# FoX attention: 128 columns in place of 256 for the scores of the first query block and the mixing of the last key block, and no zeros written

## The chip, the cores and the metric

One Trainium2 chip, one core. The metric is the device time of one execution in microseconds (us). The engines are TensorE (PE; its weight loads are listed apart as PEld), VectorE (DVE), ScalarE (ACT), GpSimd (POOL) and SyncE (SP), which issues nearly all DMAs.

## What is computed

A decoder trunk of two layers on 512 tokens of width 1024: layer 0 mixes by forgetting attention, layer 1 by a short gated convolution; each is followed by a squared-ReLU MLP and by gated per-layer embeddings, with RMSNorm around every part. The change touches the attention of layer 0 alone, with 16 heads of width 64 and query blocks of 128:

```python
c = lax.cumsum(log_f, axis=1).transpose(0, 2, 1)
def q_block(i):
    start = i * Q_BLOCK
    ...
    s = jnp.einsum('bhqd,bhkd->bhqk', qb, k, preferred_element_type=jnp.float32)
    s = s + cb[..., :, None] - c[..., None, :]
    s = jnp.where(k_pos[None, :] <= q_pos[:, None], s, NEG_INF)
    pr = jax.nn.softmax(s, axis=-1)
    return jnp.einsum('bhqk,bhkd->bhqd', pr.astype(v.dtype), v)
```

Everything is float32. The mask is causal: query block b sees keys 0 to 128(b+1), and key block j is seen by queries 128j to 512.

## The kernel before, in words

Every float32 operand of a matmul is split in two float32r parts, a rounded one (hi, written by ScalarE at L272) and a residue (lo, written by VectorE, or POOL, at L273); a product is then three matmuls (L264 to L266). In the attention the pieces are stacked so that two matmuls do:

- `scores(h, b)` (L516 on) multiplies query block b of head h with the keys. The stationary operand is the 128 queries, the moving one the keys: `kh` at L524 and `kl` at L525. Only the first n = 128(b+1) columns are wanted, but at least 256 are computed. VectorE adds bias and mask and finds the extremum (L527), ScalarE takes the exponential (L531), VectorE the reciprocal of the sum (L532), POOL multiplies by it (L533).
- `turn(h, j)` transposes the probabilities of key block j for the query blocks j to 3 (L540) and splits them into `ph` and `pl` (L272, L273). For key block 3 only columns 384 to 512 exist. POOL writes zeros to columns 256 to 384 of both (L547), for the mix reads at least 256 columns.
- `mix(h, j)` multiplies the values of key block j (stationary) with `ph` (L562) and `pl` (L563) and accumulates over j in one PSUM bank `ps_o`.

The main loop goes over c, four steps to a head: at each step `turn` for head c//4 and key block c%4, `mix` two steps behind, and `scores` eight steps ahead. Between them it deals out matmuls of the projections of later heads (`qk`) and, in the last heads, of the output projection (`o0_0`, `o1_0` and so on: column half and token block). Weight tiles (`wh`, `wl`) are split ahead of their use, eight tiles ahead as a rule (SOON) and one for the output projection (O_SOON). A scheduler with a timing model of its own then sets the order of the instructions on each engine, save in the last two steps, where TensorE keeps the order of the program. Each engine takes its own queue strictly in order. Bias rows come by DMA (`neg_c`, L510) and POOL masks their diagonal blocks (L511).

At L423, ahead of the attention, the cumulative sum over the tokens is a chain of eight float32r matmuls with a stationary operand of 16 columns and 512, 384, 256 and 128 moving ones.

Of the kernel before, what the change touches and what calls it, by code (L numbers as in the profile page):

```python
# [8 lines left out]
F32 = mybir.dt.float32  # L9
# [6 lines left out]
P = 128  # L16
D = 1024
S = 512
# [4 lines left out]
NB = S // P  # L23
# [45 lines left out]
def trunk(ctx: ExitStack, tc, x, pT, g, wv, wqk, bf, wo, wci, wcq, cw, wco, wup, wdn, wpp, wpg, out):  # L69
    nc = tc.nc  # L70
# [9 lines left out]
    def page(name, dtype=F32):  # L80
        return pages.tile([P, S], dtype, tag="pg", name=name)

    def bank(name):
        return psum.tile([P, S], F32, tag="ps", name=name)

    def stat(name, n=1, dtype=F32):
        return small.tile([P, n], dtype, tag=f"st{n}", name=name, bufs=32 if n == 1 else 8)
# [182 lines left out]
    def split(hi, lo, src, eng=nc.vector):  # L270

        nc.scalar.copy(hi, src)  # L272
        eng.tensor_tensor(out=lo, in0=src, in1=hi.bitcast(F32), op=ALU.subtract)  # L273
# [114 lines left out]
    def attention(hT, first_x, g0, by_hand):  # L388
# [127 lines left out]
        def scores(h, b):  # L516

            q, kh, kl = stacked[h // 2][h % 2]
            n = (b + 1) * P
            nm = max(n, 256)  # L520
            pr = probs[h][b]
            ps = bank(f"sc{h}_{b}")
            qb = q[:, b * P : n]
            nc.tensor.matmul(ps[:, :nm], qb, kh[:, :nm], start=True, stop=False)  # L524
            nc.tensor.matmul(ps[:, :nm], qb, kl[:, :nm], start=False, stop=True)  # L525
            nmx, sm, rs = (stat(f"{s}{h}_{b}") for s in ("nmx", "sm", "rs"))
            nc.vector.tensor_tensor_reduce(  # L527
                out=pr, in0=ps[:, :n], in1=pr, scale=-1.0, scalar=3e38, op0=ALU.add,
                op1=ALU.min, accum_out=nmx,
            )  # L530
            nc.scalar.activation(pr, pr, AF.Exp, bias=nmx, scale=-1.0, accum_out=sm)  # L531
            nc.vector.reciprocal(rs, sm)  # L532
            nc.gpsimd.tensor_scalar(out=pr, in0=pr, scalar1=rs, scalar2=None, op0=ALU.mult)  # L533
# [3 lines left out]
        def turn(h, j):  # L537
            ps = bank(f"pT{h}_{j}")
            for b in range(j, NB):
                nc.tensor.transpose(  # L540
                    ps[:, b * P : (b + 1) * P], probs[h][b][:, j * P : (j + 1) * P], ident
                )
            lo_q = min(j * P, S - 256)
            ph, pl = page(f"ph{h}_{j}", F32R), page(f"pl{h}_{j}", F32R)
            if lo_q < j * P:
                for z in (ph, pl):
                    nc.gpsimd.memset(z[:, lo_q : j * P].bitcast(F32), 0.0)  # L547
            split(ph[:, j * P : S], pl[:, j * P : S], ps[:, j * P :])
            weights[h, j] = (ph, pl)

        def mix(h, j):

            e = h % 2
            if j == 0:
                mixed[h] = bank(f"ps_o{h}")
                if e == 0:
                    outs[h // 2] = page(f"oT{h // 2}")
            ps_o = mixed[h]
            lo_q = min(j * P, S - 256)
            v = vs[j][h // 4][:, h % 4 * P : (h % 4 + 1) * P]  # L560
            ph, pl = weights.pop((h, j))
            nc.tensor.matmul(ps_o[:, lo_q:], v, ph[:, lo_q:S], start=j == 0, stop=False)  # L562
            nc.tensor.matmul(ps_o[:, lo_q:], v, pl[:, lo_q:S], start=False, stop=j == NB - 1)  # L563
            if j == NB - 1:
                a, b = slice(64 * e, 64 * e + 64), slice(64 - 64 * e, 128 - 64 * e)
                o2 = page(f"o2{h}")
                nc.scalar.copy(o2[a, :S], ps_o[b, :])
                nc.vector.tensor_tensor(
                    out=outs[h // 2][a, :S], in0=ps_o[a, :], in1=o2[a, :S], op=ALU.add
                )  # L570
                if e == 1:
                    complete.append(h // 2)
                    split_o()
# [4 lines left out]
        def split_o():  # L578

            if streaming:  # L580
                return
            if not oT:
                oT.append(turned_x)
            while complete:
                k = complete.pop(0)
                split(oT[0].hi[:, k, :], oT[0].lo[:, k, :], outs.pop(k)[:, :S])
# [77 lines left out]
        for c in range(-8, n_sc + LAG):  # L664
            if c == n_sc - BY_HAND:
                by_hand.enter_context(tc.manual_schedule(engines={E.PE}))
            share = 2 * (c + 9) if c < n_sc - 16 else 112 + (c - n_sc + 17) * (28 - LEFT) // (15 + LAG)
            while done < share + AHEAD:
                next(main, None)
                done += 1  # L670
            if 0 <= c < n_sc:
                turn(c // 4, c % 4)
            if c >= LAG:
                mix((c - LAG) // 4, (c - LAG) % 4)
            if c + 8 < n_sc:
                scores((c + 8) // 4, c % 4)
            if c % 4 == 0 and 1 < (c + 8) // 4 + LEAD < H:
                bias((c + 8) // 4 + LEAD)
# [428 lines left out]
```

## Time and profile before

| | |
|---|---|
| median of 3 runs | 1237.49 us (1236.93 to 1237.6) |
| profiled execution, span from first to last instruction | 1235.8 us |
| TensorE busy | 1213.4 us, 98% |
| stage of the change, 78 to 232 us | 154 us, TensorE busy 151.01 |
| zeros on POOL (L547) | 32 instructions, 6.4 us |

The profiled execution shows its span alone; no time of its own around the span is listed, so the median of the runs stands for it. A row of the timeline gives start and duration in us, the engine, the line, the operation, the tiles (out<-in, buffer numbers left out), the stationary shape where there is one, the shape written, and in brackets idle time before it and who ended it. Matmuls overlap, so what one costs TensorE is the step from its start to the next start. In the `out<-in` of a matmul the moving operand stands first, the stationary one second. A row of the table of stages gives the stretch and its length, then the busy time and number of instructions of PE, PEld, DVE, ACT and POOL, the granted clock, the DMA share and GB/s.

### The profile page before, as it was taken

What the parts mean: (1) busy time and instruction counts of PE and PEld (TensorE: products, weight loads), DVE (VectorE), ACT (ScalarE), POOL (GpSimd) and SP (SyncE); (2) the same over time, 40 slices, a digit from 0 to 9 for tenths busy, and PEclk for the clock granted to TensorE, in tenths of its full rate; (3) what the DMA queues carried; (4) which work ended last, traced back from release to release, by engine and by line L of the source; (5) the groups of instructions that cost most, each with busy time, mean ns of one, the idle gap of its engine ahead of it and who ended that gap; (6) DMA issues with size and microseconds to landing.
All of it is one profiled execution on the core that took longest, in us unless ns stands there. A gap on an engine that the chain in (4) does not pass through costs nothing.

```text
span 1235.8 us, 18684 instructions
## 1 busy us (share of the span) xinstructions
PE 1213.4 (98%) x6188; PEld 1030.6 (83%) x6188; DVE 896.5 (73%) x1394; ACT 676.1 (55%) x1429; POOL 686.8 (56%) x667
## 2 busy tenths in 40 slices
PE   7999999999999999999999999999999999999997
PEld 6888888888888888888889999989778888888885
DVE  5657878675667667869877798865767787669873
ACT  5457777556635654465566544445756345635551
POOL 2016667247878777775213255317778868778210
PEclk9999999999999999999999999999999999999999
DMA  7456564442343224428133033552412443235401
GB/s 253 150 160 169 147 159 114 151 164 66 115 137 98 88 88 136 123 69 288 67 102 107 27 107 96 154 176 71 136 59 78 137 136 95 66 114 178 163 18 52
DMA packets 85793, 148.73 MB, mean 120 GB/s; under 512 B 10112, under 2 KB 17328, under 8 KB 85696
## 3 DMA queue, kind: packets, MB, share of 16 engines
q1 hardware_dynamic: 85488, 147.27, 38.7%
q8 instruction: 49, 0.80, 0.3%
q14 instruction: 48, 0.39, 0.1%
q10 hardware_dynamic: 144, 0.26, 0.1%
q0 software_dynamic: 64, 0.00, 0.0%
HBM read 136.93 MB, written 6.37 MB: 116 GB/s over the span
## 4 chain that ended last, share of the span: by engine, by line
PE 89%; DVE 3%; POOL 2%; ACT 2%; issue 2%; DMA 2%; SPq 0%; POOLq 0%; DVEq 0%; ACTq 0%
PE up L266 9%; PE up L265 9%; PE up L264 9%; PE dn L265 8%; PE dn L266 8%; PE dn L264 8%; PE pg L265 2%; PE pg L264 2%; PE pg L266 2%; PE qk L264 2%; PE qk L265 2%; PE qk L266 2%; PE co L264 1%; PE co L266 1%; PE co L265 1%
## 5 line engine op out<-in xcount | busy, mean ns | idle before, releaser
L273 DVE TENSOR_TENSOR wl<-raw,wh 128x512 fp32r<-128x512 f32 (+1 forms) x398 | 370.2, 975 | 27.5 <-ACT wh L272 26.3
L272 ACT CAST wh<-raw 128x512 fp32r<-128x512 f32 (+1 forms) x398 | 217.1, 620 | 4.6 <-DVE xd L348 4.4
L265 PE MATMUL up<-hTh,wl 128*128 128x512 f32 (+1 forms) x576 | 210.2, 365 | 0.0
L266 PE MATMUL up<-hTl,wh 128*128 128x512 f32 (+1 forms) x576 | 209.7, 366 | 0.3 <-DVE hTl L273 0.3
L264 PE MATMUL up<-hTh,wh 128*128 128x512 f32 (+1 forms) x576 | 209.4, 366 | 0.0
L273 POOL TENSOR_TENSOR wl<-dn_T,wh 128x512 fp32r<-128x512 f32 x112 | 155.0, 1417 | 32.6 <-ACT wh L272 32.6
L825 ACT ACTIVATE r<-up 128x512 f32<-128x512 f32 (+1 forms) x72 | 39.4, 547 | 200.4 <-PE up L266 200.4
L871 DVE TENSOR_TENSOR acc<-dn,acc 128x512 f32<-128x512 f32 x168 | 107.2, 678 | 23.9 <-PE dn L266 23.9
L265 PEld LDWEIGHTS up<-hTh,wl 128*128 128x128 f32 x576 | 108.6, 189 | 17.7
L264 PEld LDWEIGHTS up<-hTh,wh 128*128 128x128 f32 x576 | 108.6, 189 | 17.5
L266 PEld LDWEIGHTS up<-hTl,wh 128*128 128x128 f32 x576 | 108.3, 189 | 17.9 <-DVE hTl L273 0.5
L167 POOL TENSOR_TENSOR dn_T<-raw,raw 128x512 f32<-128x512 f32 x56 | 87.5, 1575 | 58.9 <-DMA raw<-in_wdn 39.6
L167 POOL TENSOR_TENSOR dn_T<-raw,dn_T 128x512 f32<-128x512 f32 x56 | 93.3, 1666 | 2.2
L272 ACT CAST wh<-dn_T 128x512 fp32r<-128x512 f32 x112 | 61.4, 616 | 11.0 <-POOL dn_T L167 11.0
L273 DVE TENSOR_TENSOR A12l<-q,A12h 128x512 fp32r<-128x512 f32 x28 | 23.3, 833 | 51.7 <-ACT A12h L272 51.7
L273 DVE TENSOR_TENSOR A11l<-q,A11h 128x256 fp32r<-128x256 f32 x28 | 25.9, 926 | 45.5 <-ACT A11h L272 45.5
L878 POOL TENSOR_TENSOR acc<-acc,acc 128x512 f32<-128x512 f32 x28 | 46.9, 1706 | 9.9 <-DVE acc L871 9.9
L264 PE MATMUL qk<-hTh,wh 128*128 128x512 f32 x128 | 51.1, 399 | 0.0
L266 PE MATMUL qk<-hTl,wh 128*128 128x512 f32 x128 | 50.8, 397 | 0.0
L265 PE MATMUL pg<-wh,hTl 128*128 128x512 f32 x128 | 50.5, 394 | 0.0
L264 PE MATMUL pg<-wh,hTh 128*128 128x512 f32 x128 | 50.4, 394 | 0.0
L265 PE MATMUL qk<-hTh,wl 128*128 128x512 f32 x128 | 50.2, 393 | 0.0
(372 smaller groups left out, 3240.3 us busy)
## 6 DMA issues: line engine op xcount, KB each, us to landing
raw<-in_wup SPq DMA_DIRECT2D x128, 256.0 KB, 3.0
raw<-in_wdn SPq DMA_DIRECT2D x128, 256.0 KB, 2.9
raw<-in_wcq SPq DMA_DIRECT2D x36, 256.0 KB, 2.9
raw<-in_wqk SPq DMA_DIRECT2D x32, 256.0 KB, 3.6
raw<-in_wpg SPq DMA_DIRECT2D x32, 256.0 KB, 4.0
g<-in_g SPq DMA_DIRECT2D x22, 256.0 KB, 5.8
prl<-neg_c SPq DMA_DIRECT2D x16, 256.0 KB, 7.0
raw<-in_wo SPq DMA_DIRECT2D x16, 256.0 KB, 4.0
```

Of the source, the lines that this page charges most:

```text
L167: ins = nc.gpsimd.tensor_tensor(out=B[name], in0=B[a], in1=B[b], op=op)
L264: nc.tensor.matmul(ps, a.hi, b.hi, start=start, stop=False)
L265: nc.tensor.matmul(ps, a.lo, b.hi, start=False, stop=False)
L266: nc.tensor.matmul(ps, a.hi, b.lo, start=False, stop=stop)
L272: nc.scalar.copy(hi, src)
L273: eng.tensor_tensor(out=lo, in0=src, in1=hi.bitcast(F32), op=ALU.subtract)
L825: nc.scalar.activation(r[:, :n], ps[:, :n], AF.Relu)
L871: nc.vector.tensor_tensor(out=a, in0=banks[s], in1=a, op=ALU.add)
L878: nc.gpsimd.tensor_tensor(out=a, in0=a, in1=acc[i, s][:, :S], op=ALU.add)
```

## The change

The score matmuls of query block 0 and the mixing matmuls of key block 3 take 128 columns, and the zeros are not written.

```diff
             n = (b + 1) * P
-            nm = max(n, 256)
...
-            nc.tensor.matmul(ps[:, :nm], qb, kh[:, :nm], start=True, stop=False)
-            nc.tensor.matmul(ps[:, :nm], qb, kl[:, :nm], start=False, stop=True)
+            nc.tensor.matmul(ps[:, :n], qb, kh[:, :n], start=True, stop=False)
+            nc.tensor.matmul(ps[:, :n], qb, kl[:, :n], start=False, stop=True)
...
-            lo_q = min(j * P, S - 256)
             ph, pl = page(f"ph{h}_{j}", F32R), page(f"pl{h}_{j}", F32R)
-            if lo_q < j * P:
-                for z in (ph, pl):
-                    nc.gpsimd.memset(z[:, lo_q : j * P].bitcast(F32), 0.0)
...
-            lo_q = min(j * P, S - 256)
+            q0 = j * P
...
-            nc.tensor.matmul(ps_o[:, lo_q:], v, ph[:, lo_q:S], start=j == 0, stop=False)
-            nc.tensor.matmul(ps_o[:, lo_q:], v, pl[:, lo_q:S], start=False, stop=j == NB - 1)
+            nc.tensor.matmul(ps_o[:, q0:], v, ph[:, q0:S], start=j == 0, stop=False)
+            nc.tensor.matmul(ps_o[:, q0:], v, pl[:, q0:S], start=False, stop=j == NB - 1)
```

Lines behind the edits move up: L524 and L525 become L523 and L524, L540 becomes L539, L562 and L563 become L557 and L558. The scheduler then sets some instructions in another order. Three places follow, first before and then after the change; the last number of each name is only a count.

TensorE, mix of head 6, key blocks 2 and 3 (`ph6_2` to `pl6_3`), with scores of head 9 and transpositions of head 7; before:

```order
L563 MATMUL ps_o6_2166<-pl6_2_2163,v2_1_141 128x256
L524 MATMUL sc9_1_2272<-kh4_1_1720,qs4_1_1719 128x256
L525 MATMUL sc9_1_2272<-kl4_1_1721,qs4_1_1719 128x256
L562 MATMUL ps_o6_2166<-ph6_3_2189,v3_1_145 128x256
L563 MATMUL ps_o6_2166<-pl6_3_2190,v3_1_145 128x256
L540 MATMUL pT7_2_2292<-ident_75,prr7_1789 128x128
```

And after:

```order
L558 MATMUL ps_o6_2154<-pl6_2_2151,v2_1_141 128x256
L557 MATMUL ps_o6_2154<-ph6_3_2177,v3_1_145 128x128
L523 MATMUL sc9_1_2258<-kh4_1_1714,qs4_1_1713 128x256
L558 MATMUL ps_o6_2154<-pl6_3_2178,v3_1_145 128x128
L524 MATMUL sc9_1_2258<-kl4_1_1715,qs4_1_1713 128x256
L539 MATMUL pT7_2_2278<-ident_75,prr7_1781 128x128
```

The mix of key block 3 stands two and one matmuls earlier, between the scores of head 9; the set of matmuls is the same.

POOL at the zeros of head 6, which stand behind the normalizing of head 8's third query block (`prr8`) and ahead of the fourth's (`prl8`); before:

```order
L533 TENSOR_SCALAR pr4_1936<-pr4_1936,rs8_1_2134 128x256
L533 TENSOR_SCALAR prr8_1938<-prr8_1938,rs8_2_2175 128x384
L547 MEMSET ph6_3_2189 128x128
L547 MEMSET pl6_3_2190 128x128
L533 TENSOR_SCALAR prl8_1937<-prl8_1937,rs8_3_2202 128x512
```

And after:

```order
L511 AFFINE_SELECT prl9_2074<-prl9_2074 128x128
L532 TENSOR_SCALAR pr4_1926<-pr4_1926,rs8_1_2122 128x256
L532 TENSOR_SCALAR prr8_1928<-prr8_1928,rs8_2_2163 128x384
L532 TENSOR_SCALAR prl8_1927<-prl8_1927,rs8_3_2188 128x512
L511 AFFINE_SELECT prr10_2222<-prr10_2222 128x128
```

The two zeros are gone, and nothing else on POOL is moved there.

VectorE in the last heads, where residues of the output weights (`wl63`, `wl64`) stand among the softmax steps of head 15 (`ISA` is the row of L527); before:

```order
L273 TENSOR_TENSOR pl13_3_3160<-pT13_3_3157,ph13_3_3159 128x128
L273 TENSOR_TENSOR wl63_3178<-raw63_3179,wh63_3177 128x512
L532 RECIPROCAL rs15_1_3114<-sm15_1_3113 128x1
L527 ISA prr15_2971,nmx15_2_3141<-sc15_2_3138,prr15_2971 128x384
L527 ISA nmx15_2_3141 128x1
L273 TENSOR_TENSOR pl14_0_3192<-pT14_0_3186,ph14_0_3191 128x512
L273 TENSOR_TENSOR wl64_3198<-raw64_3199,wh64_3197 128x512
L532 RECIPROCAL rs15_2_3143<-sm15_2_3142 128x1
L527 ISA prl15_2970,nmx15_3_3170<-sc15_3_3167,prl15_2970 128x512
```

And after:

```order
L273 TENSOR_TENSOR pl13_3_3134<-pT13_3_3131,ph13_3_3133 128x128
L531 RECIPROCAL rs15_1_3088<-sm15_1_3087 128x1
L526 ISA prr15_2947,nmx15_2_3115<-sc15_2_3112,prr15_2947 128x384
L526 ISA nmx15_2_3115 128x1
L273 TENSOR_TENSOR wl63_3150<-raw63_3151,wh63_3149 128x512
L273 TENSOR_TENSOR pl14_0_3164<-pT14_0_3158,ph14_0_3163 128x512
L531 RECIPROCAL rs15_2_3117<-sm15_2_3116 128x1
L526 ISA prl15_2946,nmx15_3_3142<-sc15_3_3139,prl15_2946 128x512
L526 ISA nmx15_3_3142 128x1
L273 TENSOR_TENSOR wl64_3170<-raw64_3171,wh64_3169 128x512
```

Each residue stands one softmax step later.

## Prediction

> **What bounds the kernel now.** I began with the head of the page: its span, the busy times, the granted clock and the shares of the chain that ended last.
>
> ```profile
> span 1235.8 us, 18684 instructions
> PE 1213.4 (98%) x6188; PEld 1030.6 (83%) x6188; DVE 896.5 (73%) x1394; ACT 676.1 (55%) x1429; POOL 686.8 (56%) x667
> PEclk9999999999999999999999999999999999999999
> PE 89%; DVE 3%; POOL 2%; ACT 2%; issue 2%; DMA 2%; SPq 0%; POOLq 0%; DVEq 0%; ACTq 0%
> ```
>
> TensorE is busy for 98% of the span, at its full granted clock in every slice, and carries 89% of the chain. A change is therefore worth what it takes from TensorE's own time, plus what it takes from TensorE's few waits. POOL is busy for 56%, so zeros that it no longer writes count only where somebody waited for them.
>
> Next I cut out the stage of the change, from just before the first scores to the last mix, with the table of stages.
>
> ```profile
> 78.00:232.00 154.00, 151.01 (x808) 127.77 (x808) 120.64 (x340) 111.39 (x277) 97.96 (x152) 1.00 0.54 141
> ```
>
> The columns are PE, PEld, DVE, ACT and POOL. TensorE is busy for 151.0 of 154 us here, so most of its matmuls simply follow one another, and about 3 us of idle time is all that shorter waits could give.
>
> **The matmuls that get shorter.** There are 64: for each of 16 heads the two score matmuls of query block 0 (L524, L525) and the two mixing matmuls of key block 3 (L562, L563), each 256 columns before and 128 now. The group rows say 281 to 320 ns for such a 256-column matmul, but those durations overlap; the cost to TensorE is the step from one start to the next. I read it from the timeline of PE, first where three 256-column score matmuls stand together.
>
> ```profile
> 81.58 0.28 PE L525 MATMUL sc<-kl,qs 128*128 128x256 f32 x1
> 81.69 0.28 PE L524 MATMUL sc<-kh,qs 128*128 128x256 f32 x1
> 81.81 0.28 PE L525 MATMUL sc<-kl,qs 128*128 128x256 f32 x1
> 81.94 0.34 PE L524 MATMUL sc<-kh,qs 128*128 128x384 f32 x1
> ```
>
> From 81.58 to 81.94 three of them take 0.36 us: 0.12 us each. No 128-column matmul of this type with a 128x128 stationary operand stands in the trace. The nearest is the cumulative sum at L423, with a stationary operand of only 16 columns; its rows on PE, then the weight loads beside it.
>
> ```profile
> 47.96 0.22 PE L423 MATMUL ps_c<-tri,lf_h 128*16 128x128 f32 x1
> 48.02 0.22 PE L423 MATMUL ps_c<-tri,lf_l 128*16 128x128 f32 x1
> 48.08 0.44 PE L264 MATMUL v<-wh,hTh 128*128 128x512 f32 x1
> 48.36 0.39 PE L265 MATMUL v<-wh,hTl 128*128 128x512 f32 x1
> 48.59 0.39 PE L266 MATMUL v<-wl,hTh 128*128 128x512 f32 x1
> ```
>
> ```profile
> 48.02 0.19 PEld L264 LDWEIGHTS v<-wh,hTh 128*128 128x128 f32 x1
> 48.13 0.19 PEld L265 LDWEIGHTS v<-wh,hTl 128*128 128x128 f32 x1
> ```
>
> This gives both ends. The stream itself is short: 0.06 us from 47.96 to 48.02, again to 48.08, so 128 columns run at full speed. But the next matmul has 128x128 weights. Their load began with the second short matmul, at 48.02, and the following load could begin only at 48.13; the 512-column matmul recorded at 48.08 took 0.28 us to the next start, where its neighbour took 0.23. The missing 0.05 us is a load that the short stream does not cover. So a 128-column matmul followed by a 128x128 load costs the load: 0.11 us. A second place says the same, where a 128-column transposition runs ahead of a score matmul.
>
> ```profile
> 104.80 0.19 PEld L524 LDWEIGHTS sc<-kh,qs 128*128 128x128 f32 x1
> 104.91 0.19 PEld L525 LDWEIGHTS sc<-kl,qs 128*128 128x128 f32 x1
> ```
>
> Again 0.11 us from load to load. In the attention every matmul has a stationary operand of 128 columns (queries, values, normalized tokens, probabilities), so each of the 64 stands ahead of such a load. The bounds are 0.06 us (no load in the way) and 0.11 us; I take 0.11, the row with the same neighbour. **Gain: 64 x (0.12 - 0.11) = 0.64 us**; by the other end 64 x 0.06 = 3.84 us. Halving the columns is worth almost nothing by itself.
>
> The Trainium skill, "TensorE: Matmul & The Clock Gate", section "Back-to-back issue gap", gives about 81 ns per matmul for a stream of load and matmul pairs at 128 columns; by it the sum of this part would be 64 x 0.039 = 2.5 us, an estimate from that page. The rows above, 0.11 us from load to load, do not agree with it.
>
> **The zeros.** POOL writes them with 32 instructions (L547), here in groups.
>
> ```profile
> L547 POOL MEMSET pl<- 128x128 f32 x16 | 3.2, 203 | 0.0
> L547 POOL MEMSET ph<- 128x128 f32 x16 | 3.2, 203 | 0.0
> ```
>
> They go. Off POOL's 97.96 busy us that alone is nothing, but the mix of key block 3 needs both zeroed strips, and the strips are queued behind POOL's normalizing of a later head (L533). Three times TensorE came to that mix first. PE around head 1:
>
> ```profile
> 113.43 0.27 PE L540 MATMUL pT<-ident,prr 128*128 128x128 f32 x1
> 113.46 0.37 PE L563 MATMUL ps_o<-pl,v 128*128 128x256 f32 x1
> 113.67 0.27 PE L540 MATMUL pT<-ident,prl 128*128 128x128 f32 x1
> 114.49 0.39 PE L562 MATMUL ps_o<-ph,v 128*128 128x256 f32 x1 [0.56 <-POOL ph L547]
> 114.72 0.28 PE L524 MATMUL sc<-kh,qs 128*128 128x256 f32 x1
> ```
>
> A transposition and a 256-column matmul normally take 0.24 us together (113.43 to 113.67). Here they took 1.05 (113.67 to 114.72): 0.81 us lost. Heads 6 and 10:
>
> ```profile
> 161.15 0.28 PE L525 MATMUL sc<-kl,qs 128*128 128x256 f32 x1
> 162.01 0.39 PE L562 MATMUL ps_o<-ph,v 128*128 128x256 f32 x1 [0.59 <-POOL ph L547]
> 162.24 0.31 PE L563 MATMUL ps_o<-pl,v 128*128 128x256 f32 x1
> ```
>
> ```profile
> 198.85 0.28 PE L563 MATMUL ps_o<-pl,v 128*128 128x256 f32 x1
> 199.70 0.39 PE L562 MATMUL ps_o<-ph,v 128*128 128x256 f32 x1 [0.58 <-POOL ph L547]
> 199.93 0.27 PE L540 MATMUL pT<-ident,prr 128*128 128x128 f32 x1
> ```
>
> Two 256-column steps normally take 0.23 us (81.58 to 81.81). Here 1.09 and 1.08: 0.86 and 0.85 us lost. What POOL did ahead of the first:
>
> ```profile
> 113.05 1.24 POOL L533 TENSOR_SCALAR prr<-prr,rs 128x384 f32<-128x384 f32 x1
> 114.24 0.20 POOL L547 MEMSET ph<- 128x128 f32 x1
> ```
>
> The zeros waited for a 1.24 us normalization with which they have nothing to do. What would be late next? The probabilities themselves: VectorE's 128x128 residue is the last other input of that mix.
>
> ```profile
> 110.88 0.28 DVE L273 TENSOR_TENSOR pl<-pT,ph 128x128 fp32r<-128x128 f32 x1
> 158.08 0.29 DVE L273 TENSOR_TENSOR pl<-pT,ph 128x128 fp32r<-128x128 f32 x1 [0.29 <-ACT ph L272]
> 198.10 1.22 DVE L273 TENSOR_TENSOR pl<-pT,ph 128x256 fp32r<-128x256 f32 x3
> ```
>
> For heads 1 and 6 it ends at 111.16 and 158.37, 2.5 us and more before TensorE arrives. For head 10 it is the middle one of three merged instructions, which end at 199.32 at the latest; the new order takes only the rounded part right after 198.85 and the residue after two transpositions, so at most some 0.1 us could remain. The whole wait should go. **Gain: 0.81 + 0.86 + 0.85 = 2.52 us**, between 0 (another wait takes their place) and 2.52.
>
> **Moved instructions.** With the zeros gone, the scheduler sets the mix of key block 3 one or two matmuls earlier in most heads, as the order at head 6 shows; the same matmuls, so the sum of their steps stays, and the inputs lie 2.5 us back. On ScalarE, VectorE and SyncE a few weight splits and loads move behind steps of the softmax; weights are prepared up to eight tiles ahead of their use, and in the last heads, where it is one tile, the matmuls that use them move back too. So I cost this at nothing. If that cover were gone, a late weight would stop TensorE for one 128x512 split, well under 1 us each.
>
> **Sum.** 0.64 + 2.52 = 3.16 us. The span of 1235.8 goes to about 1232.6. What lies around the span is 1237.49 - 1235.8 = 1.7 us by the median of the runs; it stays. Forecast: 1237.49 - 3.16 = **1234.3 us**.
>
> **Rivals.** *The waits come back later.* TensorE, 2.5 us ahead, could run into the softmax of the last heads, where the other engines set the pace.
>
> ```profile
> 205.00:210.00 5.00, 5.00 (x32) 4.22 (x31) 2.23 (x8) 2.02 (x6) 3.25 (x7) 1.00 0.39 110
> 210.00:215.00 5.00, 4.57 (x28) 3.50 (x28) 4.88 (x16) 4.92 (x14) 5.00 (x9) 1.00 0.02 3
> 215.00:220.00 5.00, 5.00 (x28) 3.97 (x28) 5.00 (x17) 4.46 (x14) 3.90 (x4) 1.00 0.46 115
> ```
>
> For it: from 210 to 220 VectorE is busy for 9.88 of 10 us, and no gain can be had within that. Against it: from 205 to 210 VectorE is busy for 2.23 of 5, so it enters the stretch without a backlog, and the stretch begins when TensorE gets there; it should move forward as a whole. With all waits given back only the 0.64 stays: 1236.9 us; with half, 1235.6. Chance 0.24.
>
> *The load is hidden after all*, so that each short matmul costs 0.06: 3.84 + 2.52 = 6.36 us, 1231.1 us. For it speaks L423, against it the load steps. The Trainium skill, "TensorE: Matmul & The Clock Gate", section "Back-to-back issue gap", has about 56 ns at 128 columns for the gap of a matmul by itself, which would bring the same. Chance 0.09.
>
> *Short streams run at a quarter of the speed*, a reason that a padding to 256 could have had: 128 columns would then cost what 512 do, 0.23 us (48.36 to 48.59). 64 x (0.23 - 0.12) = 7.0 us more, less 2.52: 1242.0 us, slower. It would outweigh the waits from a step of 0.16 us on. L423 speaks against it: the whole piece from 47.96 to 48.36 has no room for two steps of 0.23 and a 512-column matmul. But its stationary operand is narrow. Chance 0.06.
>
> *The new order makes waits of its own* in the last heads, about as large as those removed; 0.06, half of it slower. That the change does not do what it says is excluded by the order: 128-column rows, no zeros.
>
> **How the numbers follow.** The forecast case has 0.55 and by itself reaches from 1233.5 to 1235.6. A measurement of this kernel tells about 0.2%, 2.5 us, from no change, so faster means below 1235.0: 0.45 of the forecast case and the 0.09 of the hidden load, 0.54. Within: 0.10 of the forecast, the 0.24 given back, 0.03 of the new waits, 0.37. Slower: 0.06 + 0.03 = 0.09. The range runs from the hidden load to all waits given back, 1231.1 to 1237.0; only the slower cases and some edges are left out.
>
> **What would show it.** Right: no wait of L557 on POOL in the new profile; steps of about 0.11 us after 128-column score matmuls; some 3 us less from 78 to 232, and the stages behind unchanged in length. Wrong: steps of 0.06 or 0.23; new waits of the mix or of transpositions on VectorE or POOL; a stretch from 205 on that is longer by what was won before it.

## The result, and the profile after

The change takes 1234.32 us (median of 8 runs, 1234.01 to 1235.64); the kernel before takes 1237.55 us (8 runs, 1236.93 to 1239.45). The ratio is 0.9976 (0.9967 to 0.9984): 3.2 us, or 0.24%, less. In a second series on another chip it was 1234.40 against 1237.16 us, ratio 0.9978 (0.9968 to 0.9987). The forecast was 1234.3.

The head of the page after, and the stage of the change, which is now 151 us long instead of 154:

```profile
span 1232.3 us, 18654 instructions
PE 1211.7 (98%) x6188; PEld 1029.5 (84%) x6188; DVE 898.9 (73%) x1394; ACT 676.6 (55%) x1429; POOL 680.3 (55%) x635
PE 91%; DVE 3%; ACT 2%; POOL 2%; DMA 1%; issue 1%; SPq 0%; DVEq 0%; POOLq 0%; ACTq 0%
```

```profile
78.00:229.00 151.00, 149.50 (x810) 126.67 (x808) 120.61 (x340) 111.82 (x277) 90.91 (x120) 1.00 0.56 144
```

TensorE is idle for 1.5 of these 151 us, where it was for 3.0 of 154. POOL has 32 instructions fewer and 6.5 us less to do, which nobody would notice if nobody had waited for it. Who did, the waits of the weight loads between 78 and 232 us tell, first before and then after (total, times, longest):

```profile
PEld ps_o L562 <- POOL ph L547: 2.4, 3, 0.8
PEld ps_o L562 <- DVE pl L273: 1.1, 1, 1.1
PEld pT L540 <- DVE pl L273: 0.6, 1, 0.6
```

```profile
PEld ps_o L557 <- DVE pl L273: 1.3, 2, 1.1
PEld pT L539 <- DVE pl L273: 0.8, 1, 0.8
```

The row of three waits on POOL is gone, and nothing of its size has come in its place; the waits on VectorE stood there before as well, 1.1 and 0.6 us long. In place of the third wait (head 10), PE now reads:

```profile
196.07 0.28 PE L524 MATMUL sc<-kl,qs 128*128 128x256 f32 x1
196.19 0.29 PE L558 MATMUL ps_o<-pl,v 128*128 128x256 f32 x1
196.31 0.22 PE L557 MATMUL ps_o<-ph,v 128*128 128x128 f32 x1
196.37 0.29 PE L539 MATMUL pT<-ident,prr 128*128 128x128 f32 x1
```

No idle time stands in brackets ahead of the short L557: the matmul that was held up by 0.85 us starts 0.12 us after its forerunner.

The short score matmuls hold a trap for the reader. The first scores of the stage, PE and then its weight loads:

```profile
81.06 0.22 PE L523 MATMUL sc<-kh,qs 128*128 128x128 f32 x1
81.12 0.28 PE L524 MATMUL sc<-kl,qs 128*128 128x128 f32 x1
81.23 0.33 PE L523 MATMUL sc<-kh,qs 128*128 128x256 f32 x1
81.41 0.28 PE L524 MATMUL sc<-kl,qs 128*128 128x256 f32 x1
81.52 0.34 PE L523 MATMUL sc<-kh,qs 128*128 128x384 f32 x1
```

```profile
81.07 0.19 PEld L524 LDWEIGHTS sc<-kl,qs 128*128 128x128 f32 x1
81.18 0.19 PEld L523 LDWEIGHTS sc<-kh,qs 128*128 128x128 f32 x1
81.29 0.19 PEld L524 LDWEIGHTS sc<-kl,qs 128*128 128x128 f32 x1
81.41 0.19 PEld L523 LDWEIGHTS sc<-kh,qs 128*128 128x128 f32 x1
```

The first short one seems to cost 0.06 us, the second 0.11, and the 256-column matmul behind them 0.18 where 0.12 is normal. The loads beside them come every 0.11 to 0.12 us: the late load shows up in the step of a neighbour. Only the sum over a group counts. Two short and two 256-column matmuls take 0.46 us (81.06 to 81.52); four of 256 columns took 0.48 by the 0.12 of the rows before. Two short ones save 0.02 us, 0.01 each.

To see where the time goes, I subtracted the starts of the same TensorE instruction, before minus after, in single profiled executions. "Repeated" is the change profiled once more on another chip; "strip" is an experiment below, which has no zeros per head but keeps all 256-column matmuls.

| start before (us) | place | change | repeated | strip |
|---|---|---|---|---|
| 81.01 | ahead of the first changed matmul | 0.40 | 0.41 | -0.89 |
| 110.27 | ahead of the wait at head 1 | 0.57 | 0.58 | -0.89 |
| 120.38 | behind it | 1.41 | 1.42 | -0.10 |
| 157.19 | ahead of the wait at head 6 | 1.58 | 1.59 | -0.08 |
| 167.07 | behind it | 2.55 | 2.57 | 0.84 |
| 194.89 | ahead of the wait at head 10 | 2.64 | 2.65 | 0.83 |
| 204.91 | behind it | 3.54 | 3.37 | 1.64 |
| 233.44 | behind the attention | 3.51 | 3.37 | 1.15 |
| 264.92 | next stage | 3.22 | 3.15 | 1.09 |
| 484.81 | | 3.12 | 2.78 | 1.09 |
| 1186.54 | near the end | 3.16 | 2.68 | 1.07 |

There are three jumps of 0.8 to 1.0 us at the three waits, a slow drift between them, and no further gain after 205 us. From 81 to 205 us the change gains 3.14 us, 2.96 in the repeated execution; behind that it gives back 0.38 and 0.69 us.

### The profile page after: what moved, and what is told of

Read it like the earlier page. It is cut to its first block, busy times and chain, and to the rows that moved or that the text cites. A ratio compares the mean times of both kernels' runs of the same rounds, so it can differ in the third digit from the quotient of the medians.

```text
span 1232.3 us, 18654 instructions
## 1 busy us (share of the span) xinstructions
PE 1211.7 (98%) x6188; PEld 1029.5 (84%) x6188; DVE 898.9 (73%) x1394; ACT 676.6 (55%) x1429; POOL 680.3 (55%) x635
## 4 chain that ended last, share of the span: by engine, by line
PE 91%; DVE 3%; ACT 2%; POOL 2%; DMA 1%; issue 1%; SPq 0%; DVEq 0%; POOLq 0%; ACTq 0%
PE up L266 9%; PE up L265 9%; PE up L264 9%; PE dn L265 8%; PE dn L266 8%; PE dn L264 8%; PE qk L265 2%; PE qk L264 2%; PE qk L266 2%; PE pg L265 2%; PE pg L266 2%; PE pg L264 2%; PE pT L539 1%; PE n_p L312 1%; PE co L264 1%; PE co L265 1%
## 5 line engine op out<-in xcount | busy, mean ns | idle before, releaser
L265 PE MATMUL up<-hTh,wl 128*128 128x512 f32 (+1 forms) x576 | 210.2, 365 | 0.0
L265 PEld LDWEIGHTS up<-hTh,wl 128*128 128x128 f32 x576 | 108.6, 189 | 17.5
L265 PE MATMUL qk<-hTh,wl 128*128 128x512 f32 x128 | 51.0, 399 | 0.0
L265 PE MATMUL pg<-wh,hTl 128*128 128x512 f32 x128 | 50.5, 394 | 0.0
```

Source lines behind the costliest of these rows:

```text
L265: nc.tensor.matmul(ps, a.lo, b.hi, start=False, stop=False)
```

## The experiments

My theory was the prediction's: three waits on the zeros, 2.5 us, plus 0.01 us for each of 64 matmuls. The main rival was that a short matmul costs its stream alone, 0.06 us, so that the columns would be worth six times as much and the waits little in the end. Each series has its own runs of the kernel before on its chip; the ratios go by those. Their medians run from 1236.65 to 1237.55 us, so times of different series can be compared to about 0.9 us at best.

**Scores alone, mixing alone.** The scores take 128 columns; mixing and zeros stay as before:

```diff
-            nm = max(n, 256)
+            nm = n
```

> Only the score matmuls of query block 0 take 128 columns; mix and zeros are as before the change. Theory (a short matmul costs the next weight load, 0.11 us, and the gain came from the waits on the zeros): 32 x 0.01 = 0.3 us faster than before, about 1237.2 us, and three or so waits of 0.8 us of the mix on POOL stay. Rival (the streams were the gain, 0.06 us each): 32 x 0.06 = 1.9 us faster, about 1235.6.

1236.92 us (11 runs, 1235.89 to 1237.73) against 1236.65 (27 runs): ratio 1.0003 (0.9994 to 1.0012). The lower end of the interval excludes the rival's 1.9 us; the theory's 0.32 us is within it. The trace, taken of the fastest of the eleven runs, showed something that I had not foreseen. The wait at head 1 is there, about as large as before, and so is that at head 10:

```profile
113.16 0.27 PE L540 MATMUL pT<-ident,prl 128*128 128x128 f32 x1
114.08 0.39 PE L562 MATMUL ps_o<-ph,v 128*128 128x256 f32 x1 [0.64 <-POOL ph L547]
114.30 0.28 PE L524 MATMUL sc<-kh,qs 128*128 128x256 f32 x1
```

At head 6, though, TensorE did not wait this time: the mix starts at 160.79 us, 0.13 after the score matmul ahead of it. POOL there, ahead of the zeros, first in the kernel before and then in this one:

```profile
156.44 0.29 POOL L511 TENSOR_SCALAR_AFFINE_SELECT prr<-prr 128x128 f32<-128x128 f32 x1 [1.70 <-DMA prr<-neg_c]
...
159.40 0.29 POOL L511 TENSOR_SCALAR_AFFINE_SELECT prl<-prl 128x128 f32<-128x128 f32 x1 [2.08 <-PE sc L524]
...
161.76 0.20 POOL L547 MEMSET ph<- 128x128 f32 x1
```

```profile
155.30 0.29 POOL L511 TENSOR_SCALAR_AFFINE_SELECT prr<-prr 128x128 f32<-128x128 f32 x1 [1.03 <-DMA prr<-neg_c]
...
156.88 0.29 POOL L511 TENSOR_SCALAR_AFFINE_SELECT prl<-prl 128x128 f32<-128x128 f32 x1 [0.70 <-DMA prl<-neg_c]
...
159.24 0.21 POOL L547 MEMSET ph<- 128x128 f32 x1
```

POOL waits for bias rows to land ahead of its masks, and the zeros come 2.5 us earlier when those rows do. The bracket of the second mask (`prl`) names PE in the kernel before, but the transfer that this mask reads was issued at 150.34 us and landed at 159.27, just ahead of it; with the scores alone changed it was issued at 150.00 and landed at 156.75. So how many of the three waits an execution has may well vary with the transfers. The single runs of before in this series lie 2.7 us apart, which would go with it; I did not profile several runs of one kernel to show it.

The counterpart keeps `nm = max(n, 256)` for the scores and takes the change's mixing without zeros. It keeps the change's order on every engine.

```diff
-            nc.tensor.matmul(ps[:, :n], qb, kh[:, :n], start=True, stop=False)
-            nc.tensor.matmul(ps[:, :n], qb, kl[:, :n], start=False, stop=True)
+            nc.tensor.matmul(ps[:, :nm], qb, kh[:, :nm], start=True, stop=False)
+            nc.tensor.matmul(ps[:, :nm], qb, kl[:, :nm], start=False, stop=True)
```

> The mix of key block 3 at 128 columns and no zeros as in the change, the scores of query block 0 at 256 as before; on every engine the order is that of the change. Theory (weight load bound): 32 x 0.01 = 0.3 us slower than the change, 1234.6 us. Rival (streams): 32 x 0.06 = 1.9 us slower than the change, 1236.2.

1234.83 us (11 runs) against 1236.65: ratio 0.9985 (0.9976 to 0.9994). More than half of the gain of the change comes without touching the scores. I ran it once more beside the change on one chip:

> The mix at 128 columns without zeros, scores at 256, beside the change on one chip. Theory (load bound): 0.3 us slower than the change. Rival (streams): 1.9 us slower.

> The change once more, on the same chip as the two that follow, so that their distances can be read without the spread between chips. All theories: 0.9976 of before, about 3 us less; times of single executions spread less than those of before, if the waits on the zeros come and go with the landing of the bias rows.

The change: 1234.40 us (9 runs). Mixing alone: 1234.91 (11 runs). So 32 short score matmuls are worth 0.5 us as measured, where the theory has 0.3 and the rival 1.9; single runs of each spread over some 2 us. The starts of the same instructions agree: from 81 to 205 us, where 28 of them stand, mixing alone gains 2.63 and 2.61 us in its two profiled executions, the change 3.14 and 2.96.

The expectation for the change also had a smaller spread of single times. The middle half of its runs spans 0.5 us, that of the kernel before 1.2. But the kernel with the scores alone changed, which keeps the zeros, spans only 0.6, so the spread does not show that the waits come and go.

**The cost of a short matmul by itself.** Ahead of the scores of query block 0 of every head, 16 more matmuls are issued, 256 in all; what they write is overwritten by the scores. Three kernels: 128 columns, 256 columns, and 128 columns with a stationary operand of only 64 columns.

```diff
+            if b == 0:
+                for _ in range(16):
+                    nc.tensor.matmul(ps[:128, :128], qb[:, :128], kh[:, :128], start=True, stop=True)
```

> The change with 16 extra score matmuls per head in front of those of query block 0 (their result is overwritten): 128 columns, stationary 128x128; 256 extra matmuls in all. Theory (weight load bound): 0.11 us from start to start, about 28 us more than the change. Rival (stream bound): 0.06 us each, about 15 us more; second rival (quarter speed): 0.23 us each, about 59 us more.

> The same 256 extra matmuls with 256 columns. All theories: 0.12 us from start to start, about 31 us more than the change; the difference to the 128-column ones is 0.01 us each under the load bound, 0.06 us under the stream bound.

> The same 256 extra matmuls with 128 columns, but a stationary operand of 64 columns, so that its load is half as long. Theory (the load is what bounds 128 columns): 0.06 us from start to start, about 15 us more than the change. Rival (a stream of 128 columns costs 0.11 us whatever the load): about 28 us more.

The times were 1260.87, 1263.09 and 1249.81 us (2 runs each). Against the change's first series (another chip) that is 26.5, 28.8 and 15.5 us for 256 matmuls: 0.104, 0.112 and 0.061 us each. The timelines of PE give the same from one block of 16 in each; the profile joins the 16 into one row, so the step is a sixteenth of the distance to the next start.

```profile
81.16 1.90 PE L525 MATMUL sc<-kh,qs 128*128 128x128 f32 x16
82.89 0.27 PE L526 MATMUL sc<-kh,qs 128*128 128x128 f32 x1
```

```profile
81.14 2.08 PE L525 MATMUL sc<-kh,qs 128*128 128x256 f32 x16
83.05 0.22 PE L526 MATMUL sc<-kh,qs 128*128 128x128 f32 x1
```

```profile
81.49 1.12 PE L525 MATMUL sc<-kh,qs 128*64 128x128 f32 x16
82.44 0.27 PE L526 MATMUL sc<-kh,qs 128*128 128x128 f32 x1
```

1.73/16 = 0.108, 1.91/16 = 0.119, 0.95/16 = 0.059 us. Halving the columns saves 0.011 us; halving the weights instead, with the same 128 columns, saves 0.049 and brings the step to the 0.06 us that L423 has with 16-column weights. So with 128-column weights the step of the short matmul is its weight load; the narrower operand also halves the rows written, which no run separates. Sixty-four short matmuls save 64 x 0.011 = 0.70 us, by the times of the runs 0.55. This also excludes the rival of the quarter speed (0.23 us per step).

**No zeros per head, 256 columns kept.** If the waits are what counts, zeros written once at the start must give most of the gain. The probabilities of key block 3 then go to strips of their own, whose zeros are written once. The first form has two pairs of strips, used in turn, and 68 pages instead of 70 to make room:

```diff
-PAGES = 70
+PAGES = 68
...
+        strips = [
+            tuple(consts.tile([P, 256], F32R, tag=f"z{n}{i}", name=f"z{n}{i}") for n in "hl")
+            for i in range(2)
+        ]
+        for pair in strips:
+            for z in pair:
+                nc.gpsimd.memset(z[:, :P].bitcast(F32), 0.0)
```

> All matmuls stay at 256 columns as before; the zeros are written once, ahead of the loop, into two pairs of strips used in turn (two pages fewer in the common pool to make room). Theory (waits on the zeros): about 2.5 us faster than before, 1235.0 us, no wait of the mix on POOL. Rival (shorter streams were the gain): no change, 1237.5.

1242.91 us (5 runs), ratio 1.0052 (1.0039 to 1.0065): a miss, slower by 6.3 us. By the starts of the same instructions it had gained 2.55 us up to 205 us, as expected, and then lost it elsewhere: the distance was 1.69 us at 660, -0.81 at 714, -2.46 at 840 and -5.84 at 917. The waits of PE between 650 and 920 us, here and before:

```profile
PE n_p L312 <- DVE n_h L303: 1.7, 1, 1.7
PE c L264 <- DVE za L769: 1.1, 1, 1.1
...
PE up L266 <- DVE hTl L273: 0.9, 1, 0.9
PE c L265 <- DVE wl L273: 0.6, 1, 0.6
```

```profile
PE c L264 <- DVE za L761: 0.7, 1, 0.7
PE dn L265 <- DVE S1l L273: 0.4, 1, 0.4
```

These waits are in stages which the strips do not touch; the two pages that I took away are the likeliest cause, since they leave less room to work ahead, but no run shows it by itself. The second form has one pair of strips and all 70 pages:

```diff
+        strip = [consts.tile([P, 256], F32R, tag=f"z{n}", name=f"z{n}") for n in "hl"]
+        for z in strip:
+            nc.gpsimd.memset(z[:, :P].bitcast(F32), 0.0)
...
+            if j == NB - 1:
+                ph, pl = strip
+                split(ph[:, P:], pl[:, P:], ps[:, j * P :])
+                weights[h, j] = (ph[:, :], pl[:, :])
+                return
```

> All matmuls at 256 columns as before; the zeros are written once, ahead of the loop, into one pair of 1 KB strips that all heads use in turn, and the common pool keeps its 70 pages. Theory (waits on the zeros are the gain, shorter streams 0.01 us each): 64 x 0.01 = 0.64 us slower than the change, so 2 to 2.5 us faster than before, if the free pages leave the rest alone. Rival (shorter streams, 0.06 us each): 3.8 us slower than the change, no faster than before.

1235.37 us (11 runs) against 1237.16: ratio 0.9982 (0.9974 to 0.9991), 1.8 us faster than before, a little short of the expected 2 to 2.5, and 0.97 slower than the change on the same chip, where the theory has 0.64 and the rival 3.8. PE at head 1:

```profile
114.56 0.27 PE L543 MATMUL pT<-ident,prl 128*128 128x128 f32 x1
114.59 0.36 PE L524 MATMUL sc<-kh,qs 128*128 128x256 f32 x1
114.79 0.28 PE L525 MATMUL sc<-kl,qs 128*128 128x256 f32 x1
114.91 0.28 PE L566 MATMUL ps_o<-zh,v 128*128 128x256 f32 x1
```

No wait, with 256 columns. In the table of starts its column isolates the zeros: -0.89 at 81 us to 1.64 at 205, that is 2.53 us, all in the three jumps (0.79, 0.92 and 0.81, where the prediction read 0.81, 0.86 and 0.85) and nothing between them. What the change has above that, 3.14 - 2.53 = 0.61 us (0.43 in the repeated execution), I put down to the short matmuls. Only 50 of the 64 lie in this stretch, so it is 0.012 us each (0.009), or 0.78 us (0.55) for all 64.

**The zeros written where nobody reads them.** The change, plus the 32 instructions on POOL into columns that the 128-column mix doesn't read:

```diff
+            if j == NB - 1:
+                for z in (ph, pl):
+                    nc.gpsimd.memset(z[:, S - 256 : j * P].bitcast(F32), 0.0)
```

> The change, and POOL writes the 32 zero strips all the same, though no matmul reads them. Theory (only the mix's wait mattered, not POOL's 6.4 us): as the change, 1234.3 us, within 0.5. Rival (POOL's own time was on the path of the softmax): most of the gain is lost, 1236 to 1237.5.

1235.21 us (11 runs) against 1236.65: ratio 0.9987 (0.9979 to 0.9996), 1.4 us faster than before on its chip, where the change gained 3.2 and 2.8 us in its two series, and 0.4 above mixing alone beside it. That misses my "within 0.5": about half of the gain is missing, and the rival, by which at most 1.5 us of gain would stay, is not excluded by the time.

The profiled execution (1235.08 us) shows where. By the starts of the same instructions it stands 0.38 us ahead of before at 81 us, 3.21 at 205 and 3.47 at 265, where the change has 0.40, 3.54 and 3.22. So by 265 us nothing is lost to the zeros. At 840 us both stand at 3.2 us; then 0.6 us go at 909 us in one wait of the second MLP, on a residue of VectorE (`A12l`, L265 waits 1.0 us for it instead of 0.4), where POOL writes no zeros. One execution can't tell whether this wait is the rule. Within the attention no mix waits for POOL. But the extra instructions also gave TensorE another order in over 100 rows, and the wait on VectorE at the end of the attention is longer:

```profile
224.64 0.50 PE L560 MATMUL ps_o<-ph,v 128*128 128x512 f32 x1 [1.18 <-DVE pl L273]
```

In the change it reads:

```profile
224.07 0.49 PE L557 MATMUL ps_o<-ph,v 128*128 128x512 f32 x1 [0.88 <-DVE pl L273]
```

POOL's last normalizing, which the end of the attention needs, started at 220.45 us, 1.0 later than in the change, but it was not POOL that was late; it waited itself:

```profile
220.45 1.56 POOL L532 TENSOR_SCALAR prl<-prl,rs 128x512 f32<-128x512 f32 x1 [0.74 <-DVE rs L531]
```

So POOL's time in the zeros is not what delayed that instruction. In this execution the rival does not hold; what the median's missing gain is made of, the order, the later wait or the zeros by another way, this run can't say.

**A short matmul ahead of a transposition.** Behind six of the 64 short matmuls the next instruction is a float32 transposition, not another float32r matmul. Sixteen pairs of both ahead of the first scores of each head, again overwritten:

```diff
+            if b == 0:
+                for _ in range(16):
+                    nc.tensor.matmul(ps[:, :P], qb, kh[:, :P], start=True, stop=True)
+                    nc.tensor.transpose(ps[:, P : 2 * P], ident, ident)
```

> The change with 16 extra pairs per head in front of the scores of query block 0: a 128-column score matmul, then a transposition, both overwritten; 256 pairs. A transposition's weight load shows 0.14 us where the others show 0.19. Theory (a short matmul costs what is left of the next load): ahead of a transposition it costs about 0.06 us, so a pair takes 0.11 + 0.06 = 0.17 us and all 256 some 43 us. Rival (0.11 us whatever follows): 0.22 us a pair, 56 us.

1282.88 us (2 runs): 48.5 us over the change, 0.189 us per pair. PE in the profile:

```profile
81.63 0.29 PE L526 MATMUL sc<-ident 128*128 128x128 f32 x1
81.68 0.31 PE L525 MATMUL sc<-kh,qs 128*128 128x128 f32 x1
81.83 0.30 PE L526 MATMUL sc<-ident 128*128 128x128 f32 x1
81.88 0.31 PE L525 MATMUL sc<-kh,qs 128*128 128x128 f32 x1
82.02 0.30 PE L526 MATMUL sc<-ident 128*128 128x128 f32 x1
```

0.195 us from pair to pair. A short matmul at 0.108 and a transposition at 0.11 (226.36 to 226.47 in the kernel before, one transposition behind another) would make 0.22, a free stream (0.06) 0.17; it is neither. What the pair's parts are stays open. For the sum it matters little: six such places at 0.02 us each are 0.1 us.

## Why the prediction was right

- **Shorter columns, 0.64 us.** Right: 0.55 to 0.78 us for 64 by the distance between change and strip, 0.55 to 0.70 by the blocks of 16. The choice that carried it was to take the nearest row with the same neighbour (0.11 us, a load) over the row of the stream (0.06). The sentence from the Trainium skill, "TensorE: Matmul & The Clock Gate", section "Back-to-back issue gap" (81 ns per matmul at 128 columns in a stream of load and matmul pairs), does not fit this kernel: 108 ns per float32r matmul were measured in the block of 16. The 2.5 us that the prediction estimated from it do not fit either.
- **Three waits, 2.52 us.** Right as to the cause: 2.53 us in the strip kernel. Reading the loss from the steps and not from the bracketed idle time mattered. The brackets add up to 0.56 + 0.59 + 0.58 = 1.73 us, since a matmul's recorded end lies well behind the point at which the next could start (0.28 us recorded at steps of 0.12). The prediction took all three waits as fixed, though, and that is not shown: with the scores alone changed, one of them was absent. The 2.53 us are also counted from the same execution of the kernel before from which the prediction was read, so they say what the waits came from and not how often they come; by the medians the strip kernel is 1.8 us faster.
- **Moved instructions, nothing.** Right within the attention: the gain from 81 to 205 us is explained without them. At head 10 the bound of 0.1 us on a new wait held: the mix goes on without one.
- **Waits that come back later.** They did not come back where the rival put them: from 205 to 233 us the distance goes from 3.54 to 3.51. The strip kernel lost 0.49 us there, so the place is a real one.
- **What the sum left out.** The first changed matmul already starts 0.40 us early. That stands in the kernel's very first matmul, which waits for a row brought by DMA and starts at 5.97 us instead of 6.38. Over all profiled executions it starts between 5.97 and 6.57 us, and at 6.43 in the kernel with blocks of 64-column weights, which has the change in it; so no run ties this lead to the change. (The strip kernel's 0.89 us the other way go with the clock: from 17 to 20 us its granted clock was 0.52, and matmuls of 272 columns step by 0.23 us there where the kernel before has 1.00 and 0.13.) And 0.38 us is given back after 205 us, 0.69 in the repeated execution, though the prediction had the stages behind unchanged in length. Part of it lies in a wait of the first MLP on its token residue:

```profile
PE up L266 <- DVE hTl L273: 0.6, 1, 0.6
```

It was 0.3 us before. The early start and what is given back happen to cancel, so that the hit to a tenth of a microsecond is partly luck; the terms themselves are good to some 0.2 us, and the medians of two series differ by 0.5 us in what they give the change (3.23 and 2.76).

## What to carry to other kernels

When columns are cut, ask what else sets the step: here a matmul with 128-column weights costs the next weight load, 0.108 us, and 128 columns are hardly cheaper than 256. Padding is dear by what it makes others wait for: zeros queued behind an unrelated instruction of over 1 us on another engine stopped TensorE three times in the profiled execution, and taking away the need for them, not their 0.2 us each, brought most of the gain. Sum steps over a group of matmuls rather than reading one step, since a late load appears in a neighbour's.

## What had not been expected of the hardware

- With a stationary operand of 64 columns the same 128-column matmul takes 0.059 us a step instead of 0.108, and its load is recorded with 135 instead of 192 ns.
- A short float32r matmul and a float32 transposition take 0.195 us together, less than two loads of 0.108.
- Between the two strip kernels lie some 8 us (6.3 slower than before with 68 pages, 1.8 faster with 70 and one pair), all behind the attention, in a kernel whose TensorE is busy for 98%. No run took two pages from the kernel before and nothing else.
